# A hybrid decoder block: a second delta head's operands turned by VectorE and DMA in place of TensorE, and other numbers in the ordering

## The chip, the cores and the metric

One core of one Trainium2 chip. The metric is device microseconds of one execution of the whole program. The kernel before took 626.52 us in the median of three runs (623.9 to 627.73).

## The reference

The program computes one decoder layer in float32 for 1024 positions of width 1024. After an RMS norm, one projection gives the inputs of two groups of heads that work side by side: eight heads of stick-breaking attention (width 64) and four heads of a gated delta rule (width 128). Both groups' outputs are normed per head, gated, put beside each other, multiplied by one output matrix and added to the input, and a last RMS norm follows. The part that the change touches first is the delta rule, which works on chunks:

```python
qkv = jax.nn.silu(causal_depthwise_conv(concat([g_q, g_k, g_v]), gdn_conv_w))
gq, gk = l2norm(to_heads(gq)), l2norm(to_heads(gk))
# per chunk: k_beta = k * beta, v_beta = v * beta, decay from the cumulated g
a_mat = where(strict, einsum('bhnid,bhnjd->bhnij', k_beta, k) * decay, 0)
sol = triangular_solve(a_mat + eye, [v_beta, k_beta * exp(g)])
attn_intra = where(incl, einsum('bhnid,bhnjd->bhnij', q, k) * decay, 0)
# scan over chunks: v_new = u - w S;  o = (q exp(g)) S + attn_intra v_new
# S = S exp(g_last) + (k exp(g_last - g))^T v_new
```

The other part is the norm of the attention's output, `o_sb = rmsnorm(o_sb, sb_norm_w) * silu(sb_z)`, ahead of the output product.

## The kernel before, in words

**Tiles.** Positions are cut into 8 blocks of 128, the width into 8 of 128. Every large product is made as three products of float32 parts (a high and a low part of each operand, high x high, high x low, low x high; `mm3`, line 615), each 128x128 by 128x512 where it can be.

**Stages.** First the queries of the attention and its values are projected, with the input's split into high and low parts. Then two kinds of work share TensorE: the rest of the projections, which serve as filler, and the chains of the attention heads and of the delta heads. Then comes the output: the delta group's half of the product first (`products_delta`, line 1617), block by block, then the attention's half with the last norm (`products_attention`, line 1643).

**A delta head.** The projections of k, q and v of a delta head h (names G{h}1, G{h}0 and G{h}2) come out with the channel on the partitions and the position along the free side, 512 positions at a time; `g_evac` (line 913) applies the convolution and the gate. The inner products need them in this form, but the norms, the state's update and the solve need them turned, with the position on the partitions. There are two ways to turn them, chosen by `h < TURNED` (line 32, value 2). Heads below it keep k and q on the chip: GpSimd's product writes them straight into the operand tile kq, and v is stored to DRAM (g_s) and loaded again as it is; `gdn_pre` (line 1087) then turns all three by TensorE transposes against a unit matrix into PSUM, four of 128x128 for each of k, q and v of a unit (a unit is one half of the sequence of one head, four chunks). ScalarE squares the result, VectorE copies k out of PSUM, ScalarE scales v. Heads from it on are turned on the way: VectorE transposes each 128x512 block in squares of 32 (tile tn), four DMAs store its quarters to DRAM (gt_s) so that the squares land in turned order, and k and q are also stored unturned (g_s). `delta_load` (line 1036) loads kq from g_s, and the turned k, q and v (kn, nkv, vt) from gt_s; ScalarE's squares and scaling then read SBUF. All loads and stores of these go through SyncE's queue.

**The delta chain.** `gdn_pre` of both units, `gdn_sub` (line 1159, a forward substitution on GpSimd), `gdn_inv` (line 1192, the inverse of the 128x128 triangles in steps, tile xinv) and `gdn_chain` (line 1269, the scan over chunks) follow one another for each head. Units are numbered u = 2h + g. The operand tiles have room for four units, so unit u waits for the scan of unit u - 4. A unit's load of v waits until the unit before it is through with `gdn_pre`, and the loads of the next unit's k and q come behind it.

**The output.** `enter_delta` (line 1566) asks for the delta group's output blocks and their gates (tile mg), the first four as soon as the scan of unit 6 is through, and notes block b as ("in", b, 1) in `ready`. `out_norm` (line 1463), in two streams, one for even and one for odd blocks, loads the attention's output (tile both, four DMAs per block), adds its two parts, and makes the norm's factor; `enter_attention` (line 1630) uses it once all delta blocks have been asked for.

**What sets the order.** The program is written out as some twenty streams (`interleave`, line 468; the list stands at the end of `block`). A model of the chip (`Model`, line 188) runs beside the writing: each instruction has a cost, and the time at which its result can be used elsewhere is its end plus a hop (`HOPS`, line 41: A is ScalarE, G GpSimd, P TensorE, V VectorE, S the DMAs; `TO_PE`, line 42, is added where TensorE is the reader). A stream may go on when what it waits for has ended by the model's clock plus the hop, `TO_PE` and `SLACK` (line 465):

```python
return all(o.end is not None and o.end + HOPS[o.eng] + TO_PE + SLACK <= ck.now for o in self.waits)
```

Of the streams that may go on, the one with the best priority writes its next TensorE instructions; the other engines' orders come from the model's heaps by priority. In the end each engine's instructions are tied into this order. So these numbers set no wait on the chip; they set who stands behind whom.

Of the kernel before, what the change touches and what calls it, by code (L numbers as in the profile page):

```python
# [17 lines left out]
P = 128  # L18
# [4 lines left out]
SBH = 8  # L23
# [5 lines left out]
ORDER = "G0 v1 k0 G1 k1 G2 k2 G3 k3 z4 z5 z6 z7 z0 z1 z2 z3".split()  # L29
LOADS = "k0 k1 x0 k2 x1 x2 k3 x3 x4 k4 x5 k5 x6 x7 k6 k7 c0 c1 c2 c3 s c4 c5 c6 c7".split()  # L30
WINDOWS = 3
TURNED = 2

# [2 lines left out]


SAME = 130  # L40
HOPS = {"A": 145, "G": 75, "P": 197, "V": 130, "S": 900}
TO_PE = 70
SLACK = 450
GAP = "gap"

PORT = 60
# [141 lines left out]
class Model:  # L188
# [95 lines left out]
    def hop(self, d, op):  # L284
        return SAME if d.eng == op.eng != "S" else HOPS[d.eng] + (TO_PE if op.eng == "P" else 0)

# [14 lines left out]
    def finish(self, op):  # L301
        op.end = self.now
        for u in op.users:
            self.wake(u, op.end + self.hop(op, u))
        self.at(op.end + HOPS[op.eng] + TO_PE + SLACK, lambda: None)

# [147 lines left out]
class Stream:  # L454
# [7 lines left out]
    def ready(self, ck):  # L462
        if self.gate and not self.gate():
            return False
        return all(o.end is not None and o.end + HOPS[o.eng] + TO_PE + SLACK <= ck.now for o in self.waits)

# [35 lines left out]
def block(tc, xT_d, x_d, n1_d, wE_d, wQ_d, wC_d, conv_d, alog_d, dtb_d, mixw_d, wo_d, fnw_d, out_d):  # L502
    nc = tc.nc
    ck = Model({"V": nc.vector, "A": nc.scalar, "G": nc.gpsimd, "P": nc.tensor, "S": nc.sync})
    V, A, G, TE, S = ck.V, ck.A, ck.G, ck.P, ck.S

    with ExitStack() as top:
# [7 lines left out]
        fx = Fixed(ck, nc, {**{f"sg{w}": (2048 * (w + 1), 1) for w in range(4)}, "o2": (1024, 1), "kq": (4096, 4), "ak": (4096, 4)})  # L515
# [29 lines left out]
        def rsqrt(y, a, n):  # L545
            return G.tensor_tensor(y, a, half[:, 0:n], ALU.pow)
# [33 lines left out]
        def turned(tp, parts):  # L580
            ck.hold(tp)
            for u, a in enumerate(parts):
                if a.dtype == F32R:
                    TE.transpose(tp[:, u * P:(u + 1) * P].bitcast(F32R), a, idr)
                else:
                    TE.transpose(tp[:, u * P:(u + 1) * P], a, ident)
            ck.free(tp)
            yield from ()
# [161 lines left out]
        def first(f, *args, bank=BANK, **kw):  # L750
            ck.prio, prio = bank, ck.prio
            f(*args, **kw)
            ck.prio = prio
# [49 lines left out]
        flags = {}  # L803
# [103 lines left out]
        def operand(h, g):  # L907
            if (h, g) not in operands:
                operands[h, g] = fx.tile([P, 4, 2, P], F32, "kq", "kq")
                ck.hold(operands[h, g])  # L910
            return operands[h, g]

        def g_evac(h, kind):
# [3 lines left out]
            def evac(pt, half):  # L917
# [14 lines left out]
                ts = slice(half * 512, half * 512 + 512)  # L932
                if h < TURNED and kind < 2:
                    kq = operand(h, half)
# [4 lines left out]
                first(G.tensor_tensor, ac, ac, sg, ALU.mult)  # L939
                if h < TURNED:  # L940
                    return S.dma_start(g_s[h, kind, :, ts], ac)
# [94 lines left out]
        def delta_load():  # L1036
            yield lambda: "dec" in flags
            for h in range(GH):
                for g in range(2):
# [9 lines left out]
                    for kind in (1, 0):  # L1049
                        yield lambda: f"G{h}{kind}{half}" in flags  # L1050
                        loads.append(flags[f"G{h}{kind}{half}"] if h < TURNED else S.dma_start(kq[:, :, 1 - kind, :], g_s[h, kind, :, ts].rearrange("p (c t) -> p c t", c=4)))
                    ak = fx.tile([P, 2, 4, P], F32, "ak", "ak")
# [4 lines left out]
                    turned = lambda kind: gt_s[h, kind, ts, :].rearrange("(c t) d -> t c d", t=P)  # L1057
                    if h >= TURNED:
                        loads += [S.dma_start(kn, turned(1)), S.dma_start(nkv, turned(0))]
                    flags[f"l{u}g"] = loads  # L1060
                    yield lambda: f"G{h}2{half}" in flags and (u == 0 or f"q{u - 1}" in flags)
                    vt = gd.tile([P, 4, P], F32 if h >= TURNED else F32R, tag="vt", name="vt")
                    flags[f"v{u}g"] = S.dma_start(vt, turned(2)) if h >= TURNED else S.dma_start(vt.rearrange("p c t -> p (c t)").bitcast(F32), g_s[h, 2, :, ts])
                    gst[h, g].update(vt=vt)
# [396 lines left out]
        normed = {}  # L1461

        def out_norm(n):
            yield lambda: f"e{SBH - 1}3" in flags and fx.room("sg3")
            if n == 0:
                fx.part("sg3", 4096)
            for b in range(n, NB, 2):
                yield lambda: fx.room("sg3")
                both = fx.tile([P, SBH, 2, SBD], F32, "both", "sg3")
                ck.hold(both)  # L1470
                loads = []
                for q in range(4):
                    at = 32 * (4 * (b % 2) + q)
                    loads.append(S.dma_start(both[32 * q:32 * q + 32].rearrange("p h u d -> p (h u d)").rearrange("p (n c) -> p n c", c=32),
                                             o_s[b // 2, :, :, at:at + 32].rearrange("h (a r) c -> r (h a) c", r=32)))
                yield loads
                yield lambda: ck.now > max(op.end for op in loads) + 2000
                o, spare = both[:, :, 0, :], both[:, :, 1, :]
                V.tensor_tensor(o, o, spare, ALU.add)
                A.activation(spare, o, AF.Square)  # L1480
                ss = at_.tile([P, SBH], F32, tag="oss", bufs=2, name="oss")
                V.tensor_reduce(ss, spare, AX.X, ALU.add)
                V.tensor_scalar(ss, ss, 1.0 / SBD, EPS, ALU.mult, ALU.add)
                rsqrt(ss, ss, SBH)
                normed[b] = both, o, ss
                yield
# [74 lines left out]
        ready = {}  # L1561
# [81 lines left out]
        def products_attention():  # L1643
            yield lambda: f"d{NB - 1}" in flags
            for b in range(NB):
# [3 lines left out]
                for got in product(b, 0, parts):  # L1649
# [41 lines left out]
        interleave(ck, lambda: ps.room("pz", 4),  # L1691
                   [Stream(delta_scan(), 0, DELTA), Stream(delta_solve(), 0.5, DELTA + 0.5), Stream(delta_substitute(), 0.6, DELTA + 0.6),
                    pre, Stream(delta_load(), 0.4, DELTA + 0.4), Stream(attention(), 9.995, WINDOW), Stream(attention_values(), 9.99, WINDOW), Stream(out_rows(), 9.1, OUT_WEIGHTS), Stream(out_weights(), 9, OUT_WEIGHTS), Stream(out_weights_attention(), 9.25, OUTPUT + 1), Stream(out_rest(), 9.26, OUTPUT + 1), Stream(enter_x(), 9.31, OUTPUT - 4), Stream(out_norm(0), 9.15, OUTPUT - 1), Stream(out_norm(1), 9.16, OUTPUT - 1), fill,
                    Stream(enter_delta(), 9.3, OUTPUT - 4), Stream(prepare(1), 9.2, OUTPUT), Stream(products_delta(), 101, OUTPUT - 5),
                    Stream(enter_attention(), 9.1, OUTPUT - 3), Stream(prepare(0), 9.05, OUTPUT - 2), Stream(products_attention(), 102, OUTPUT - 1.5)])
# [39 lines left out]
```

## Time and profile before

| what | value |
|---|---|
| median of three runs | 626.52 us (623.9 to 627.73) |
| the profiled execution's own time | 624.59 us |
| its span, first to last instruction | 622.9 us |
| granted TensorE clock, mean | 0.998 |
| moved by DMA | 115.99 MB, mean 186 GB/s |

The profile is one execution. Its rows give, for each engine, the busy time, and for a group of like instructions their count, total busy time, mean duration and the idle time of the engine ahead of them. PE is TensorE, PEld its weight loads, DVE VectorE, ACT ScalarE, POOL GpSimd, SPq the issuing of DMAs in SyncE's queue. Matmuls overlap: the pace of TensorE is read from one start to the next and not from durations. In the table of stages the columns are the stretch, its length, busy time and count of each engine in the order PE, PEld, DVE, ACT, POOL, then the granted clock, the DMA engines' busy share and GB/s. Nearly all instructions carry the line of the recording helper (L377), so rows are told apart by the tiles that they write and read: kwf is the operand tile read by the transposes of k and q, vt that of v, akf the turned k, pz and pp are PSUM.

### The profile page before, as it was taken

The page shows a single profiled execution, that of the slowest core. Times are in us where ns is not written, and L with a number is a line of the kernel's source. Part 1 is how long each engine was busy: PE and PEld are TensorE (multiplying, and loading weights), DVE is VectorE, ACT ScalarE, POOL GpSimd, SP SyncE. Part 2 cuts the span into 40 slices and gives each one's busy share as a digit, 9 for nine tenths or more (in the row PEclk, how much of TensorE's full clock was granted, in tenths as well). Part 3 has the DMA queues.
Part 4 walks back from the last instruction along what each step waited for, and adds up shares of the span by engine and source line. Part 5 has one row for each costly group of instructions (what it writes and reads, how often), then busy time and mean ns, then how long its engine had stood idle before and what let it go on. Part 6 is the DMA issues. An engine that isn't in the chain of part 4 may idle for free.

```text
span 622.9 us, 11147 instructions
## 1 busy us (share of the span) xinstructions
PE 611.9 (98%) x3672; PEld 518.2 (83%) x3672; DVE 445.2 (71%) x803; ACT 397.1 (64%) x971; POOL 346.6 (56%) x435
## 2 busy tenths in 40 slices
PE   8999999999999999999999999999999999999995
PEld 7889988998888888887888888788878888888785
DVE  4369983242587787889789787886998865567774
ACT  5765468833776786885878767766778743223554
POOL 0126043945887469786558796584854416325433
PEclk9999999999999999999999999999999999999999
DMA  8968234776226547678647789236454389997632
GB/s 292 336 227 316 85 124 131 255 258 218 70 87 218 175 125 210 143 199 241 188 124 209 176 234 322 74 127 197 106 155 132 113 225 257 301 234 174 162 126 102
DMA packets 162233, 115.99 MB, mean 186 GB/s; under 512 B 95168, under 2 KB 130176, under 8 KB 162176
## 3 DMA queue, kind: packets, MB, share of 16 engines
q1 hardware_dynamic: 161888, 115.09, 61.3%
q8 instruction: 29, 0.48, 0.3%
q14 instruction: 28, 0.23, 0.1%
q10 hardware_dynamic: 288, 0.20, 0.1%
HBM read 78.12 MB, written 37.13 MB: 185 GB/s over the span
## 4 chain that ended last, share of the span: by engine, by line
PE 89%; ACT 2%; DVE 2%; DMA 2%; issue 2%; SPq 1%; POOL 1%; POOLq 0%; ACTq 0%
PE pp L377 57%; PE pz L377 23%; PE po L377 6%; PE pc L377 3%; DMA xr1f<-xT 1%; SPq L377 1%; DMA br<-bd 1%; ACT ahl L377 0%; ACT wy L396 0%; DVE xr L377 0%; POOL oss L377 0%; DVE xinv L396 0%; DVE mgf L377 0%; DVE oss L377 0%; DVE tn L377 0%
## 5 line engine op out<-in xcount | busy, mean ns | idle before, releaser
L377 PE MATMUL pp<-xh,weh 128*128 128x512 f32 x360 | 145.1, 403 | 0.0
L377 PE MATMUL pp<-xh,wel 128*128 128x512 f32 x360 | 140.8, 391 | 0.0
L377 PE MATMUL pp<-xl,weh 128*128 128x512 f32 x360 | 140.7, 391 | 0.0
L377 POOL TENSOR_TENSOR sgf<-sgf,cc 128x128 f32<-128x128 f32 (+3 forms) x64 | 77.2, 1210 | 54.5 <-DVE cc L377 43.2
L377 POOL TENSOR_TENSOR wel<-wer,weh 128x512 fp32r<-128x512 f32 x48 | 63.1, 1318 | 60.1 <-ACT weh L377 58.6
L377 PEld LDWEIGHTS pp<-xh,wel 128*128 128x128 f32 x360 | 67.6, 188 | 14.9
L377 PEld LDWEIGHTS pp<-xh,weh 128*128 128x128 f32 x360 | 67.7, 188 | 12.0
L377 PEld LDWEIGHTS pp<-xl,weh 128*128 128x128 f32 x360 | 67.8, 188 | 11.8
L377 ACT ACTIVATE sgf<-pz,rs 128x384 f32<-128x384 f32 (+3 forms) x96 | 53.7, 588 | 8.1 <-PE pz L377 7.7
L377 DVE TENSOR_TENSOR ahl<-pz,ahl 128x512 fp32r<-128x512 f32 (+1 forms) x80 | 49.5, 629 | 12.6 <-ACT ahl L377 12.0
L377 DVE TENSOR_TENSOR_SCAN cc<-pz,step 128x384 f32<-128x384 f32 (+2 forms) x64 | 53.4, 844 | 6.7 <-ACT pz L377 5.1
L377 ACT ACTIVATE pz<-pz,ns 128x384 f32<-128x384 f32 (+3 forms) x96 | 52.0, 569 | 0.0
L377 ACT ACTIVATE ahl<-pz 128x512 fp32r<-128x512 f32 (+1 forms) x80 | 43.1, 555 | 12.7 <-PE pz L377 12.4
L377 PE MATMUL po<-ahl,v2a 128*128 128x512 f32 (+1 forms) x160 | 49.3, 400 | 0.0
L377 PE MATMUL pp<-wo,mmf 128*128 128x512 f32 x192 | 44.5, 391 | 0.0
L377 POOL TENSOR_TENSOR mmf<-mgf,mmf 128x512 fp32r<-128x512 f32 x16 | 21.6, 1349 | 40.2 <-ACT mmf L377 40.2
L377 DVE SCALAR_TENSOR_TENSOR pp<-pre,conv,pp 128x512 f32<-128x512 f32 x42 | 31.4, 747 | 17.1 <-ACT pp L377 16.6
L377 PE MATMUL pp<-woh,mmf 128*128 128x512 f32 (+2 forms) x136 | 41.8, 382 | 0.4 <-ACT mmf L377 0.4
L377 PEld LDWEIGHTS pp<-wo,mmf 128*128 128x128 f32 x192 | 35.8, 188 | 7.4
L377 DVE TENSOR_TENSOR_SCAN cc<-pz,cc,step 128x512 f32<-128x512 f32 (+1 forms) x32 | 38.6, 1205 | 2.4 <-ACT pz L377 1.5
L377 PE MATMUL pz<-kh,q 128*128 128x384 f32 (+3 forms) x96 | 36.0, 382 | 0.9 <-DVE cc L377 0.3
L377 DVE TENSOR_TENSOR xr<-pp,xr 128x512 f32<-128x512 f32 (+2 forms) x33 | 22.2, 672 | 20.2 <-PE pp L377 18.1
(317 smaller groups left out, 1503.0 us busy)
## 6 DMA issues: line engine op xcount, KB each, us to landing
wer<-wE SPq DMA_DIRECT2D x48, 256.0 KB, 3.7
xr<-x SPq DMA_DIRECT2D x16, 512.0 KB, 6.4
v_s<-v2e SPq DMA_DIRECT2D x16, 256.0 KB, 3.0
v2a<-v_s SPq DMA_DIRECT2D x16, 256.0 KB, 2.9
q<-qk_s SPq DMA_DIRECT2D x8, 512.0 KB, 5.7
kh<-qk_s SPq DMA_DIRECT2D x8, 512.0 KB, 4.9
kl<-qk_s SPq DMA_DIRECT2D x8, 512.0 KB, 5.8
o_s<-oe SPq DMA_DIRECT2D x32, 128.0 KB, 3.5
```

What stands on the lines that cost most here:

```text
L377: ins = f(*args, **kw).ins
```

## The change

```diff
-TURNED = 2
+TURNED = 1
...
-HOPS = {"A": 145, "G": 75, "P": 197, "V": 130, "S": 900}
-TO_PE = 70
-SLACK = 450
+HOPS = {"A": 150, "G": 75, "P": 197, "V": 120, "S": 900}
+TO_PE = 80
+SLACK = 435
...
         def out_norm(n):
-            yield lambda: f"e{SBH - 1}3" in flags and fx.room("sg3")
+            yield lambda: f"e{SBH - 1}3" in flags and fx.room("sg3") and ("in", 1, 1) in ready
```

With `TURNED` at 1, head 1 goes the way of heads 2 and 3: only head 0 is still turned by TensorE. The streams of the attention's norm start only when the delta group's output blocks 0 and 1 have been asked for. Four of the model's numbers differ, two up and two down.

## The prediction

> **What bounds the kernel now.** I read the page first (busy shares, granted clock, the chain that ended last), then the table of stages, then the timeline of TensorE around the instructions that go, then the groups by shape.
>
> ```profile
> span 622.9 us, 11147 instructions
> ...
> PE 611.9 (98%) x3672; PEld 518.2 (83%) x3672; DVE 445.2 (71%) x803; ACT 397.1 (64%) x971; POOL 346.6 (56%) x435
> ...
> PE 89%; ACT 2%; DVE 2%; DMA 2%; issue 2%; SPq 1%; POOL 1%; POOLq 0%; ACTq 0%
> ```
>
> ```profile
> 150.00:220.00 70.00, 70.00 (x454) 57.96 (x453) 49.09 (x87) 49.24 (x131) 50.34 (x69) 1.00 0.41 137
> 220.00:290.00 70.00, 69.45 (x407) 58.81 (x407) 60.30 (x107) 53.21 (x146) 55.96 (x76) 1.00 0.69 187
> ...
> 210.00:460.00 250.00, 248.49 (x1622) 209.37 (x1623) 208.03 (x383) 183.92 (x499) 176.54 (x243) 1.00 0.62 177
> ...
> 617.00:623.00 6.00, 0.00 (x0) 0.00 (x0) 0.71 (x2) 1.07 (x3) 1.12 (x2) 0.75 0.33 128
> ```
>
> TensorE is the bound: 98% busy over the span, 89% of the chain that ended last, no idle time at all from 150 to 220 us and 1.51 us of 250 from 210 to 460 us; the granted clock is 1.00 until the tail. The last 6 us, without TensorE, are the last block's norm and store, which the change leaves alone. So an edit counts by what it takes off TensorE's queue or by the stalls it makes there; work on other engines counts only if TensorE ends up waiting for it.
>
> **The change, part by part.** *Head 1's transposes leave TensorE.* The loops over heads use "h < TURNED", so with 1 in place of 2 only head 1 (units 2 and 3, its two halves of the sequence) changes its path. Per unit 4 transposes of k, 4 of q and 4 of v go, 24 in all; the rows below are those of head 1.
>
> ```profile
> 173.18 0.80 PE L377 MATMUL pz<-step,kwf 128*128 128x128 f32 x8
> 173.81 0.46 PE L377 MATMUL pp<-xh,weh 128*128 128x512 f32 x1
> ...
> 206.13 0.54 PE L377 MATMUL pz<-step,vt 128*128 128x128 f32 x4
> 206.50 0.84 PE L377 MATMUL pz<-step,kwf 128*128 128x128 f32 x8
> 207.18 0.70 PE L377 MATMUL po<-ahl,v2a 128*128 128x512 f32 x2
> ...
> 214.90 0.53 PE L377 MATMUL pz<-step,vt 128*128 128x128 f32 x4
> 215.27 0.70 PE L377 MATMUL po<-ahl,v2a 128*128 128x512 f32 x2
> ```
>
> One group's price is its start to the start of what follows, since starts show the pace and durations overlap: 173.81 - 173.18 = 0.63, 207.18 - 206.13 = 1.05, 215.27 - 214.90 = 0.37, together 2.05 us for 24, or 0.085 us each. As this stretch has no idle time, all of it is on the bounding engine: -2.05.
>
> [...]
>
> *What VectorE gets.*
>
> ```profile
> L377 DVE STREAM_TRANSPOSE tn<-ac 128x512 f32<-128x512 f32 x12 | 8.4, 698 | 0.5 <-POOL ac L377 0.5
> ...
> L377 DVE COPY akf<-pz 128x512 f32<-128x512 f32 x4 | 2.7, 683 | 0.5 <-DMA dt_s<-dtf 0.5
> ```
>
> Twelve transposes of a 128x512 block serve heads 2 and 3, six per head (three kinds, two halves). Head 1 adds six: 6 x 0.698 = 4.2 us. Two copies of the turned k out of PSUM go: 2 x 0.683 = 1.4. Net +2.8 us on VectorE, which is 49.09 of 70 busy in the stage where they fall; the cover is its 20.9 us of idle time there. ScalarE's squares and scalings are the same in number, reading SBUF in place of PSUM. GpSimd's products keep their number too.
>
> *What SyncE's queue and the DMA engines get.* Before, head 1 issues 4 DMAs (v stored and loaded twice). After: 4 stores of k and q, 24 stores of turned quarters, 4 loads of k and q, 4 of their turned forms, 2 of v: 38, so 34 more.
>
> ```profile
> g_s<-ac SPq DMA_DIRECT2D x12, 256.0 KB, 2.5
> gt_s<-tn SPq DMA_DIRECT2D x48, 64.0 KB, 2.8
> ...
> akf<-gt_s SPq DMA_DIRECT2D x4, 256.0 KB, 4.7
> ...
> L377 SPq DMA_DIRECT2D gt_s<-tn x48: 303/490/1457, 220.5 to 357.7; - x48
> ```
>
> At the median of 0.49 us for one issue this is 34 x 0.49 = 16.7 us more in the queue. Blocks go up by 16 x 256 KB = 4.2 MB; with the 9.6 MB moved from 150 to 220 (70 us at 137 GB/s) that is 13.8 MB, or 197 GB/s, near the 187 of the next stage, where heads 2 and 3 already go this way. That stage is the nearest row for all the side effects together. It shows 0.55 us of TensorE idle per 70, and slower issue of the first matmul after a wait:
>
> ```profile
> L377 PE MATMUL pp<-xh,weh 128*128 128x512 f32 x70 | 27.6, 395 | 0.0
> ...
> L377 PE MATMUL pp<-xh,weh 128*128 128x512 f32 x58 | 23.5, 406 | 0.0
> ```
>
> These are 150 to 220 and 220 to 290 us. If head 1's stage became like the next, it would lose 0.55 + 70 x 0.011 = 1.3 us; if the queue has room, 0; six freed PSUM banks (one for each group of four transposes) allow a gain, bounded by the 0 idle of the stage to nothing visible. VectorE comes to 51.9 of 70, a quarter of the way from 49.1 to 60.3, so I take a quarter: +0.3.
>
> *Is head 1 late?* Its operands now pass through DRAM.
>
> ```profile
> 188.03 1.30 POOL L377 TENSOR_TENSOR ac<-ac,pre 128x512 f32<-128x512 f32 x1
> ...
> 201.34 0.32 SPq L377 DMA_DIRECT2D vt<-g_s  x1
> ...
> 341.82 1.29 POOL L377 TENSOR_TENSOR ac<-ac,pre 128x512 f32<-128x512 f32 x1
> ...
> 350.60 0.37 SPq L377 DMA_DIRECT2D vt<-gt_s  x1
> ```
>
> From the product of v to the issue of its load it is 13.3 us in head 1 (not turned) and 8.8 in head 3 (turned), so v is no later than now. Unit 3's k and q are loaded behind unit 2's v: issue near 201.3, four issues of 0.49, landing 4.7: 208.0. Today unit 3's turning starts at 206.50 and ScalarE's squares some 0.7 later; so unit 3 is about 1 us late. The next thing that could be late is head 1's substitution, then its scan, which frees the buffers of head 3's units. Two covers stand there.
>
> ```profile
> 455.65 0.44 DVE L377 STREAM_TRANSPOSE wc<-xc 128x256 f32<-128x256 f32 x1
> ...
> 459.68 0.40 ACT L377 ACTIVATE xinv<-xc 32x256 f32<-32x256 f32 x1
> ...
> 514.85 1.28 POOL L377 TENSOR_TENSOR mmf<-mgf,mmf 128x512 fp32r<-128x512 f32 x1 [3.81 <-ACT mmf L377]
> ...
> 524.52 0.39 PE L377 MATMUL pp<-xh,wel 128*128 128x512 f32 x1
> 524.75 1.52 PE L377 MATMUL pp<-wo,mmf 128*128 128x512 f32 x6
> ```
>
> Head 3's inverse is at hand at 455.65 and used at 459.68: 4.0 us. The output's first block is split at 514.85 + 1.28 = 516.13 and TensorE, filled with projections until then, takes it at 524.75: 8.6 us. Cost of 1 us of lateness: 0; without these covers, 1.
>
> *The norms' loads wait.* The added condition holds back the first loads of the attention rows until the output's second block has been asked for.
>
> ```profile
> 502.53 0.38 SPq L377 DMA_DIRECT2D bothf<-o_s  x1
> ...
> 504.00 0.46 SPq L377 DMA_DIRECT2D bothf<-o_s  x1
> 504.51 3.22 SPq L377 DMA_DIRECT2D mgf<-og_s  x1
> ...
> 508.80 0.44 SPq L377 DMA_DIRECT2D mgf<-gate_s  x1
> ...
> L377 DVE TENSOR_TENSOR mgf<-bothf,oss x8: 681/682/1351, 539.2 to 604.1; 128x512 f32<-128x512 f32 x8
> ```
>
> Two loads stand ahead of the second block's today; they move behind 508.80, some 6.7 us later, and at most the other six loads of these two blocks with them. Queued behind the condition is only the norm's own chain, whose result is first wanted at 539.2; and the first output block comes at most 2.0 us (504.51 - 502.53) earlier into an 8.6 us wait. Both ends are covered: 0. Without cover it would be +6.7 or -2.0.
>
> *Hop times.* They are numbers of the planner that writes each engine's order, and put no instruction on the chip. The time after which a stream may go on is the sum of three: after ScalarE 145 + 70 + 450 = 665 and 150 + 80 + 435 = 665; after VectorE 650 and 635; after GpSimd 595 and 590. The order is new all the same, since 34 DMAs come and 24 transposes go. Its worth cannot be read ahead; its bound can:
>
> ```profile
> L377 PE MATMUL pp<-xh,weh 128*128 128x512 f32 x360 | 145.1, 403 | 0.0
> ...
> L377 PE MATMUL pp<-xl,weh 128*128 128x512 f32 x360 | 140.7, 391 | 0.0
> ...
> L377 PE MATMUL po<-ahl,v2a 128*128 128x512 f32 x128 | 45.5, 430 | 0.0
> ```
>
> Against 391 ns, the two slow groups lose 360 x 0.012 + 128 x 0.039 = 9.3 us, and 1.5 us of idle stand from 210 to 460: an order without a stall would gain 10.8, one twice as poor would lose as much. I take 0, as nothing points to either side.
>
> **The sum**: -2.05 + 0.3 + 0 + 0 + 0 = -1.75. The profiled execution took 624.59 (its span 622.9 and 1.7 around it), which gives 622.84. The median of the three runs is 626.52, 1.93 above it; the new one will be compared as a median, so I add half of that: 623.8.
>
> **The rivals.** *The new order pays* (B): half of the 10.8 us of stalls goes. For it: they are made of waits between engines, which the order sets. Against it: nothing in the change aims at a named one. 624.59 - 1.75 - 5.4 + 0.97 = 618.4, faster by 1.3%. *Head 1 comes late* (C), the side of slower: SyncE's queue is in order, 24 stores each wait for a VectorE transpose, and what stands behind them, head 1's own loads among them, waits too. The lateness goes from unit 3 through head 1's scan to head 3's loads and to the output's first block, and decides from 4.0 + 8.6 = 12.6 us on; from there each us costs one. At 22 us (all 16.7 of issue time and one landing of 4.7 in series) it costs 8.8: 624.59 - 1.75 + 8.8 + 0.97 = 632.6. For it: single issues of up to 1.457 us. Against it: heads 2 and 3 are served in 8.8 us. [...] *Nothing comes of it* (D): other work closes the gaps at once and TensorE waits elsewhere for as long: 624.59 + 0.97 = 625.6. Against it: no idle time around the 24.
>
> **How the numbers follow.** Forecast 0.60, B 0.20, C 0.11, D 0.09. One per cent, 6.3 us, is about what a measurement of this kernel tells from no change. B alone is faster by more, C alone slower, the other two lie within: 0.20, 0.69, 0.11. The range runs from 616.5 (B with a little more than half of its stalls) to 632.5 (C at its price); outside it I leave a third of B and half of C with the tails of the rest, under 0.2.
>
> **What would show it.** Right: the group of transposes of kwf falls from 32 to 16 and of vt from 16 to 8, the turned blocks rise from 12 to 18 and their stores from 48 to 72, TensorE's busy time falls by about 2 us with its idle time unchanged. The norms' loads stand behind the second output block, and the first product still follows the last projection without a gap. Wrong: a gap there (C); mean durations of the two slow groups moved by 10 ns or more (B, or its opposite); TensorE's busy time the same (D).

## The result, and the profile after

The changed kernel takes 629.50 us in the median of 20 runs (625.43 to 632.59), the kernel before 626.24 in as many beside it (623.6 to 628.53, and one slow run of 676.07 that the ratio leaves out): ratio 1.0056, 95% interval 1.0038 to 1.0073, so slower by 0.6%. The prediction said 623.8, and 616.5 to 632.5 as its range: the time lies within the range and on the other side of no change.

The profiled execution took 628.0 us. From its page (span, busy times, granted clock in 40 slices, the chain that ended last):

```profile
span 626.3 us, 11173 instructions
...
PE 611.0 (98%) x3648; PEld 518.4 (83%) x3648; DVE 451.4 (72%) x807; ACT 398.8 (64%) x971; POOL 345.9 (55%) x435
...
PEclk9999999999999899999999999999999999999999
...
PE 82%; DVE 7%; ACT 4%; POOL 2%; issue 2%; DMA 1%; SPq 0%; POOLq 0%; DVEq 0%; ACTq 0%
```

TensorE is 0.9 us less busy than before (611.9), and the span is 3.4 us longer, so its idle time has grown by 4.3 us: 15.3 where before had 11.0. The chain runs through VectorE for 7% of the span (2% before). And one slice of the granted clock, the fourteenth (203 to 219 us), reads 8 and not 9. The table of stages says where the idle time went. After, then before:

```profile
200.00:210.00 10.00, 7.79 (x127) 5.94 (x125) 9.24 (x20) 9.26 (x33) 6.21 (x9) 1.00 0.60 144
210.00:220.00 10.00, 9.88 (x55) 8.07 (x55) 6.08 (x16) 4.65 (x14) 2.35 (x6) 0.83 0.58 196
...
400.00:410.00 10.00, 8.32 (x126) 6.18 (x126) 9.00 (x20) 7.75 (x19) 5.75 (x6) 1.00 0.32 89
470.00:490.00 20.00, 18.55 (x175) 15.13 (x174) 18.23 (x32) 15.76 (x40) 8.88 (x9) 1.00 0.38 111
515.00:600.00 85.00, 85.00 (x400) 70.49 (x399) 55.85 (x88) 30.02 (x61) 36.07 (x27) 1.00 0.83 224
```

```profile
200.00:210.00 10.00, 10.00 (x133) 8.35 (x132) 7.75 (x17) 8.46 (x34) 4.03 (x8) 1.00 0.76 256
...
400.00:410.00 10.00, 9.77 (x53) 8.18 (x54) 8.97 (x17) 6.61 (x17) 7.60 (x11) 1.00 0.44 143
470.00:490.00 20.00, 19.86 (x113) 16.22 (x111) 17.25 (x32) 15.33 (x37) 10.02 (x8) 1.00 0.28 94
515.00:600.00 85.00, 84.46 (x389) 69.29 (x388) 56.41 (x88) 30.86 (x57) 37.36 (x29) 1.00 0.83 216
```

Three short stretches hold most of it: 2.2 us of TensorE's idle time at 200 to 210 (none before), 1.7 at 400 to 410 (0.2 before), 1.45 at 470 to 490 (0.1). The output has none. The three are the inverses of heads 0, 2 and 3. At the first of them VectorE (third busy column) has gone from 7.75 to 9.24 of 10 us, and the ten us behind it have a granted clock of 0.83.

The timeline shows it instruction by instruction. The inverse passes three times from TensorE to VectorE and back: TensorE's first products (wc, dt) are copied into y, the second (xc, y) into wy and xinv, and the third (wy, dt) read these. VectorE after, at head 0's inverse:

```profile
205.23 0.86 DVE L377 COPY y<-pz 32x256 f32<-32x256 f32 x2
206.12 1.22 DVE L377 TENSOR_TENSOR_SCAN cc<-pz,step 128x512 f32<-128x512 f32 x1
207.38 0.42 DVE L377 COPY wy<-pz 32x256 f32<-32x256 f32 x1
207.81 0.85 DVE L377 COPY xinv<-pz 32x256 f32<-32x256 f32 x2
```

and TensorE after:

```profile
207.62 0.28 PE L377 MATMUL pz<-kl,q 128*128 128x256 f32 x1
208.80 0.69 PE L377 MATMUL pz<-wy,dt 128*64 128x64 f32 x16 [0.90 <-DVE xinv L377]
210.12 0.50 PE L377 MATMUL pp<-xh,weh 128*128 128x512 f32 x1 [0.64 <-DVE kt L377]
210.46 0.39 PE L377 MATMUL pp<-xl,weh 128*128 128x512 f32 x1
210.69 0.46 PE L377 MATMUL pp<-xh,wel 128*128 128x512 f32 x1
210.95 0.63 PE L377 MATMUL pp<-xh,weh 128*128 128x512 f32 x1
211.38 0.63 PE L377 MATMUL pp<-xl,weh 128*128 128x512 f32 x1
...
213.94 0.56 PE L377 MATMUL pp<-xl,weh 128*128 128x512 f32 x1
214.34 0.39 PE L377 MATMUL pp<-xh,wel 128*128 128x512 f32 x1
```

VectorE goes from one instruction to the next without a pause, an attention scan of 1.22 us stands ahead of the copies, and TensorE's third products wait for them (the bracket: idle time and what ended it). Then comes what the page's 8 stands for: from 210.95 to 213.94 the same 128x512 products start 0.43 us apart where they start 0.23 apart before and after it. The granted clock is 0.50 for 3.4 us there (210.90 to 214.30), which costs an estimated 1.7 us (half of 3.4). Before, VectorE had pauses there, and TensorE had head 1's transposes to run ahead of the second products (the rows from 206.13 to 207.18 that the prediction shows) and twelve projection products behind them. VectorE, then TensorE, before:

```profile
206.25 0.86 DVE L377 COPY y<-pz 32x256 f32<-32x256 f32 x2 [0.53 <-PE pz L377]
...
208.57 0.42 DVE L377 COPY wy<-pz 32x256 f32<-32x256 f32 x1 [0.98 <-PE pz L377]
209.00 0.85 DVE L377 COPY xinv<-pz 32x256 f32<-32x256 f32 x2
```

```profile
208.44 0.54 PE L377 MATMUL pz<-step,stf 128*128 128x128 f32 x4
208.81 0.46 PE L377 MATMUL pp<-xh,weh 128*128 128x512 f32 x1
...
211.43 0.39 PE L377 MATMUL pp<-xh,wel 128*128 128x512 f32 x1
211.75 0.69 PE L377 MATMUL pz<-wy,dt 128*64 128x64 f32 x16
```

So VectorE's results are not later than before: the copies of xinv end at 208.66 after and at 209.85 before. TensorE comes to them sooner. Between its second and its third products it has two small ones after (from 207.40 and 207.62 on) and sixteen before, so after the change it stands ready for xinv at 207.90 and waits, while before it came to it at 211.75.

**The clock goes with the time.** The mean granted clock of the 20 runs lies between 0.986 and 0.997, mean 0.9915; in 23 runs of the kernel before it is 0.9973. One stretch of 3.4 us at 0.50 in 627, as in the profiled run, lowers the mean by 0.0027; by this estimate the lower mean is worth some two such stretches in a run (the profiled run, at 0.995, has one). (0.9973 - 0.9915) x 629.5 = 3.7 us, where the medians differ by 3.3: by this estimate the change would be worth about -0.4 us without these stretches. The 20 runs are one kernel in one order, and their times go with their clocks: the five at 0.995 or more took 625.4 to 628.3 us, the seven at 0.989 or less 630.3 to 632.0. A run with longer waits may have both, so this alone does not say what the clock costs by itself.

### The profile page after: what moved, and what is told of

Same layout as the page of the kernel before. It is cut to its first block, busy times and chain, and to the rows that moved or that the text cites. A ratio compares the mean times of both kernels' runs of the same rounds, so it can differ in the third digit from the quotient of the medians.

```text
span 626.3 us, 11173 instructions
## 1 busy us (share of the span) xinstructions
PE 611.0 (98%) x3648; PEld 518.4 (83%) x3648; DVE 451.4 (72%) x807; ACT 398.8 (64%) x971; POOL 345.9 (55%) x435
## 4 chain that ended last, share of the span: by engine, by line
PE 82%; DVE 7%; ACT 4%; POOL 2%; issue 2%; DMA 1%; SPq 0%; POOLq 0%; DVEq 0%; ACTq 0%
PE pp L377 55%; PE pz L377 20%; PE po L377 5%; PE pc L377 3%; DVE cc L377 2%; DMA wq<-wQ 1%; ACT sgf L377 1%; POOL sgf L377 1%; ACT pz L377 1%; DVE ahl L377 1%; POOL tm L377 0%; ACT akf L377 0%; POOL xs L377 0%; DVE pp L377 0%; POOL wel L377 0%
## 5 line engine op out<-in xcount | busy, mean ns | idle before, releaser
L377 PE MATMUL pp<-xh,weh 128*128 128x512 f32 x360 | 146.6, 407 | 0.6 <-DVE kt L377 0.6
L377 PE MATMUL po<-ahl,v2a 128*128 128x512 f32 (+1 forms) x160 | 47.9, 396 | 0.0
L377 DVE TENSOR_TENSOR xr<-pp,xr 128x512 f32<-128x512 f32 (+2 forms) x33 | 22.2, 673 | 21.2 <-PE pp L377 20.9
```

The lines of the kernel that those rows point to most:

```text
L377: ins = f(*args, **kw).ins
```

## The experiments

Theory 1: TensorE's short waits at the delta heads' inverses, bunched within some microseconds, are followed by half-clock stretches, and these are the loss. Theory 2: the half clock has another origin and the new order costs the time as work and waits on the path; or any new order falls where it falls. All numbers are medians; every ratio is against the kernel before on the same chip. "Busy" is TensorE's busy time between 203 and 213 us in the run's own profile, around head 0's inverse (in e10 and e10b its third products start only at 220.85 and 216.19 us). "Between" is the number of products that TensorE has there between the inverse's second and third products, fillers included, by each run's timeline.

| kernel | TURNED | other | us | ratio, 95% interval | clock | busy | between |
|---|---|---|---|---|---|---|---|
| before | 2 | old hops, slack 450 | 626.24 | 1 | 0.998 | 10.00 | 16 |
| changed | 1 | new hops, slack 435, gate | 629.50 | 1.0056 (1.0038 to 1.0073) | 0.991 | 7.67 | 2 |
| e1 | 1 | as before | 644.38 | 1.0282 (1.0247 to 1.0318) | 0.990 | 8.08 | 2 |
| e2 | 2 | new hops, 435 | 628.51 | 1.0036 (1.0017 to 1.0055) | 0.997 | 10.00 | 20 |
| e4 | 1 | new hops, 435, no gate | 635.64 | 1.0145 (1.0112 to 1.0178) | 0.989 | 7.60 | 2 |
| e7 | 2 | before + 24 transposes | 626.23 | 1.0006 (0.9986 to 1.0027) | 0.997 | 10.00 | 16 |
| e8 | 1 | changed + 24 filler products | 630.33 | 1.0078 (1.0060 to 1.0097) | 0.998 | 8.95 | 6 |
| e9 | 2 | before + 24 filler products | 629.78 | 1.0071 (1.0047 to 1.0095) | 0.998 | 10.00 | 20 |
| e11 | 1 | changed + 8 filler products | 629.57 | 1.0055 (1.0030 to 1.0081) | 0.993 | 8.22 | 4 |
| e12 | 2 | before + late copies | 630.43 | 1.0061 (1.0036 to 1.0086) | 0.995 | 10.00 | 16 |
| e10 | 1 | changed, solves 800 ns later | 635.32 | 1.0162 (1.0139 to 1.0186) | 0.991 | 5.94 | 14 |
| e10b | 2 | before, solves 800 ns later | 637.09 | 1.0184 (1.0165 to 1.0203) | 0.988 | 10.00 | 10 |
| a 425 | 1 | changed, slack 425 | 628.57 | 1.0041 (1.0017 to 1.0065) | 0.994 | 7.66 | 2 |
| a 440 | 1 | changed, slack 440 | 629.67 | 1.0063 (1.0036 to 1.0091) | 0.991 | 7.86 | 2 |
| a 450 | 1 | changed, slack 450 | 636.59 | 1.0159 (1.0116 to 1.0203) | 0.985 | 7.56 | 2 |
| a 460 | 1 | changed, slack 460 | 637.85 | 1.0196 (1.0164 to 1.0228) | 0.992 | 7.34 | 0 |
| b 440 | 2 | before, slack 440 | 635.48 | 1.0145 (1.0099 to 1.0192) | 0.998 | 9.97 | 20 |
| b 445 | 2 | before, slack 445 | 623.97 | 0.9965 (0.9942 to 0.9989) | 0.997 | 10.00 | 16 |
| b 455 | 2 | before, slack 455 | 627.21 | 1.0021 (0.9998 to 1.0044) | 0.998 | 10.00 | 16 |
| e13 | 1 | changed, head 1's turns as copies | 629.66 | 1.0063 (1.0043 to 1.0083) | 0.993 | 8.03 | 2 |

### The parts of the change

e1 has the turning alone, e2 the numbers of the ordering alone, e4 both without the gate. The gate by itself has no run: added to the kernel before, to e1 or to e2, it leaves every engine's written order as it is. Only with TURNED at 1 and the new numbers together does it move instructions. So e2 is also the changed kernel with TURNED at 2.

```diff
# e1
-TURNED = 2
+TURNED = 1
# e2
-HOPS = {"A": 145, "G": 75, "P": 197, "V": 130, "S": 900}
-TO_PE = 70
-SLACK = 450
+HOPS = {"A": 150, "G": 75, "P": 197, "V": 120, "S": 900}
+TO_PE = 80
+SLACK = 435
# e4: both
```

> The change's first part alone: head 1 turned by VectorE, old hop times, no gate. Theory (order): the loss of the changed kernel is made of stalls where the new order puts the inverse's matmuls of a delta head too close behind the VectorE copies that they read, and of half-clock windows of 3.4 us that follow such stalls; it hangs on the order, so this kernel, with another order, may come out anywhere from 1.75 us below the kernel before (stalls as before) to 4 us above. Rival (turning): the added VectorE and queue work costs 3 us whatever the order: 629 to 630 us, as the changed kernel, with waits in the stretch from 160 to 220 us. A clock of 0.997 or more with a time under 626 speaks for the order, one of 0.992 or less with a time near 629.5 for either, and then the place of the waits decides.

> The hop times alone: head 1 still turned by TensorE. Theory (order): another order of the same work, so the time moves by the stalls it happens to make, within 4 us of the kernel before to either side, and the granted clock tells how many half-clock windows it met, about 1.5 us for each 0.0027 of mean clock. Rival (turning): hop times are harmless, ratio 1.000 within 0.002.

> Head 1 turned by VectorE and the new hop times, without the gate on the norms' loads. Both theories: as the changed kernel, ratio 1.0056 within 0.003, if the gate does nothing until the output; the waits at the inverse near 205 to 210, 404 to 408 and 478 to 481 us stand there again. If it is level with the kernel before or faster, the gate has a price after all, of 3 us.

The turning alone costs 18 us, far outside what either theory gave it. TensorE's longest wait in e1 (us in all, times, the longest), and the stage with it:

```profile
PE pp L377 <- POOL wel L377: 4.3, 1, 4.3
```

```profile
365.00:380.00 15.00, 10.72 (x54) 8.78 (x53) 8.48 (x13) 5.45 (x18) 13.01 (x15) 0.89 0.79 260
```

With the old numbers, the order that comes out of TURNED = 1 has TensorE wait 4.3 us in one piece for a weight's low part from GpSimd at 371 us, and a clock of 0.89 over these 15 us. In all TensorE is idle for 23.4 us in e1 (11.0 before), and three slices of its granted clock read 8 (0.991 in the mean of the profiled run). The new numbers take 8.7 us off (644.38 to 635.64), the gate another 6.1 (to 629.50). This too was not expected (ratio 1.0056 within 0.003). In e4 the last attention rows are asked for at 599.5 us (594.1 in the changed kernel), and the last block waits for its halves. Two of TensorE's waits there, and the stage:

```profile
605.69 0.50 PE L377 MATMUL pp<-woh,mmf 128*128 128x512 f32 x1 [1.24 <-ACT mmf L377]
...
607.34 1.22 PE L377 MATMUL pp<-woh,mmf 128*128 128x512 f32 x2 [0.92 <-POOL mmf L377]
```

```profile
600.00:612.00 12.00, 9.82 (x41) 7.42 (x40) 7.41 (x15) 5.57 (x11) 5.46 (x5) 0.86 0.45 125
```

That is 2.2 us of idle time and a clock of 0.86 over the 12 us; in the changed kernel TensorE has no idle time from 590 to 612. It is not the whole of the 6.1 us, and the clock on record does not follow e4's times throughout: one of its six runs shows 0.943 and is the fastest, 632.94 us. So the small edits mend orders that the first one upset; alone, the numbers cost 2.3 us (e2), with the clock at 0.997 and TensorE's waits in the output (busy for 81.49 of 85 us from 515 on). Set against e2, which differs in TURNED alone, the changed kernel is slower by 0.0056 - 0.0036 = 0.0020, or 1.3 us (-0.4 to 2.9): with these numbers the turning's own share is not clear of nothing.

### Does the removed work count?

e7 issues each of head 1's 24 transposes twice, in the order of the kernel before.

```diff
                     for which in range(2):
+                        if h == 1:
+                            nc.tensor.transpose(tp[...], kw[:, j, which, :], idr)
...
+                    if h == 1:
+                        nc.tensor.transpose(bank[...], vt[:, j, :], idr)
```

> The kernel before with each of head 1's 24 transposes on TensorE issued twice, every engine's order otherwise the same. It measures the term of 2.05 us by itself: on the path that sets the end, 2.0 us more, ratio 1.0033; hidden by waits, ratio 1.000. The first copies have names of their own line in the profile.

The pairs start 0.085 us apart, as the prediction read it, yet 24 more cost 0.4 us at the end (-0.9 to 1.7), and not 2.05. Its stage is as full as before's (the row of before stands in the prediction), so what they take there must be given back later in the run; where, no run shows.

```profile
150.00:220.00 70.00, 70.00 (x469) 58.31 (x468) 48.27 (x85) 48.35 (x129) 48.75 (x68) 1.00 0.42 135
```

### Filling the waits

e8 and e9 put two 512-column products ahead of the inverse's first product into its PSUM bank and four ahead of the next, which overwrite their results; the planner doesn't know of them, so the order stays. e11 has two per inverse, both in the second place.

```diff
             x1p = pz()
+            for _ in range(2):
+                nc.tensor.matmul(x1p, idr, stepr, start=True, stop=True)
...
             y2p = pz()
+            for _ in range(4):
+                nc.tensor.matmul(y2p, idr, stepr, start=True, stop=True)
```

> The changed kernel with six extra 512-column matmuls per delta head at the head's inverse (two ahead of the first product into the inverse's bank, four ahead of the second's), their results overwritten: 24 matmuls, 5.4 us of TensorE work at 0.227 us each, put where TensorE waits for VectorE's copies. Theory 1 (short waits bunched at the inverses are followed by 3.4 us at half clock, each worth 1.7 us, about two and a half of them in a run): the mean clock goes from 0.991 back to 0.996 or more and the time falls from 629.5 us to 625.5 to 628, below the changed kernel in spite of the added work. Theory 2 (the half-clock stretches have another origin): the clock stays near 0.991 and the time is 629.5 to 635. Theory 3 (the changed order is slower by work on the path, the clock is only a companion): the time rises by the added 2 to 5.4 us whatever the clock does.

> The same 24 extra matmuls in the kernel before, whose mean clock is 0.998: the control that prices them. Theory 1: no half-clock stretches are there to be saved, the clock stays at 0.997 to 0.998, and the time rises by 2 to 5.4 us to 628 to 631.6, less what falls into waits. Theory 2 and 3: the same rise as in the changed kernel.

> The changed kernel with only two extra 512-column matmuls per inverse, ahead of the product that waits for the second copies (8 in all, 1.8 us at 0.227 us each; in the kernel before the 24 of the earlier run cost 3.9 us, so 8 cost about 1.3). Theory 1 (the lost time is half-clock stretches behind bunched waits): they fill the longest wait of the bunch; the mean clock rises to 0.995 or more from 0.991, and the time is 626.5 to 628. Theory 2 (a companion): clock 0.991, time 630 to 631.

The clock does what theory 1 says: back to 0.998 from 0.991 in the changed kernel, unchanged in the kernel before. Two stretches of 3.4 us at head 0's inverse, in e8:

```profile
207.50:210.90 3.40, 2.35 (x60) 1.68 (x62) 2.33 (x6) 3.18 (x18) 2.50 (x4) 1.00 0.77 223
210.90:214.30 3.40, 3.40 (x30) 2.56 (x26) 1.90 (x4) 2.52 (x7) 1.18 (x5) 1.00 1.01 270
```

and in the changed kernel:

```profile
207.50:210.90 3.40, 1.86 (x21) 1.44 (x22) 2.46 (x6) 3.34 (x16) 2.78 (x6) 1.00 0.95 256
210.90:214.30 3.40, 3.40 (x9) 2.64 (x8) 1.25 (x2) 1.77 (x6) 0.32 (x2) 0.50 0.98 324
```

TensorE busy for 1.86 of 3.4 us is followed by a clock of 0.50, busy for 2.35 by 1.00. The time did not fall to 625.5 to 628, as I had expected it to: the filler costs more than it mends, 0.0071 x 626 = 4.4 us in the kernel before. In the changed kernel it costs 0.0078 - 0.0056 = 0.0022, or 1.4 us. The 3.1 us between them (0.9 to 5.3, from the three intervals) are what the filler mends in the changed kernel and not in the kernel before. That is not the clock alone, since waits shrink too: by the pages TensorE's idle time falls from 15.3 to 12.5 us in e8 and rises from 11.0 to 12.5 in e9. The clock by itself (0.9915 to 0.9968 in the mean) would give 3.3 as an estimate; these runs do not part the two. With the filler on both sides the change costs 0.0007 x 626 = 0.4 us (-1.5 to 2.3). e11's eight products raise the clock to 0.993 only; its two longest bunches stay, and the time with them. My expectation for it failed: the filler ran behind the wait and not within it. The two products at head 0 start at 208.78, after 0.89 us of waiting for xinv; in e8 the four in the second place start at 209.60, after 1.05.

### Making the kernel before late

```diff
+            for _ in range(3):
+                nc.vector.tensor_copy(W[32:64, :, 0:32], xv[32:64])
             r = V.tensor_copy(W[32:64, :, 0:32], xv[32:64])
```

> The kernel before with VectorE's copy of the second product made four times in place of once (three more, 0.42 us each, 1.26 us per inverse), unknown to the planner, so that every result behind it on VectorE lands 1.3 us late, as in the changed kernel where VectorE has no pause at 200 to 208 us. Theory 1 (late copies at the inverses make TensorE wait in bunches, and half clock follows): the clock falls from 0.998 to 0.988 to 0.994, and the time rises to 629 to 636: up to 1.3 us of waiting at each of four inverses, and 1.7 us for each half-clock stretch. Theory 2 (the half-clock stretches have another origin): clock 0.998, and the time rises by no more than the waits, 0 to 5 us.

```profile
290.00:298.00 8.00, 6.24 (x90) 4.83 (x89) 7.34 (x16) 5.42 (x13) 0.40 (x2) 1.00 0.88 285
394.00:400.00 6.00, 4.88 (x85) 3.43 (x83) 5.08 (x14) 2.59 (x7) 1.28 (x1) 1.00 0.22 55
462.00:469.00 7.00, 5.42 (x63) 4.28 (x58) 6.79 (x16) 5.45 (x15) 2.52 (x5) 1.00 0.12 31
```

```profile
290.00:298.00 8.00, 7.29 (x95) 5.67 (x95) 7.57 (x15) 5.78 (x14) 0.90 (x3) 1.00 0.85 252
394.00:400.00 6.00, 6.00 (x104) 4.67 (x104) 4.64 (x12) 3.78 (x10) 1.28 (x1) 1.00 0.26 68
462.00:469.00 7.00, 6.58 (x62) 4.83 (x61) 5.77 (x12) 6.09 (x15) 1.87 (x3) 1.00 0.35 73
```

The first fence is e12, the second the kernel before. Copies 1.3 us late add about 1.1 us of idle time at each of the last three inverses, 3.3 in all; head 0's inverse, with its filler at hand, takes none (busy 10.00 in the table). The time rises by 0.0061 x 626 = 3.8 us, which the waits all but account for, and the clock falls from 0.997 to 0.995, just short of the 0.988 to 0.994 that theory 1 asked for. The bunches are 1.1 to 1.8 us of idle time here, smaller than at head 0 in the changed kernel (2.2); so the clock's sign is theory 1's, and the effect weaker than I had set it; the time alone lies within theory 2's 0 to 5 us as well. Its profiled run, at 0.999, lost 0.001 x 627 = 0.6 us to the clock, less than the 1.7 of one half-clock stretch.

### The solves later in the order

e10 and e10b ask for 800 ns more ahead of every step of the solves.

```diff
+        self.slack = SLACK + (800 if prio == 0.5 else 0)
-        ... + TO_PE + SLACK <= ck.now for o in self.waits)
+        ... + TO_PE + self.slack <= ck.now for o in self.waits)
```

> The changed kernel, with the solves' products put 800 ns later in the written order behind what they wait for than the model asks, so that other products stand where TensorE now waits at the inverses. Theory 1 (the waits come from results that land later than the model has them, and are followed by half-clock stretches): the mean clock is 0.995 or more, and the time 625 to 628. Theory 2 (any new order falls anywhere within some per cent): the time lies anywhere between 622 and 640, and the clock goes with it.

> The kernel before with the same 800 ns in its solves. Theory 1: few such waits were there, so the clock stays at 0.997 to 0.998 and the time within 2 us of 626.2, unless the later solves make the output wait. Theory 2: anywhere between 622 and 640 us.

Both are slower than the kernel before by ten us or more: my expectations for theory 1 failed in both. The waits went elsewhere, in both to the output's start. e10b:

```profile
520.00:541.00 21.00, 14.82 (x49) 11.29 (x48) 10.03 (x16) 5.59 (x19) 6.37 (x7) 0.59 0.65 189
```

6.2 of 21 us idle at the output's start, and a clock of 0.59 over them: 17 us at half speed. Heads that come out later are paid for there, as the prediction's rival C had it, though here it is the solves that were put off.

### Is it the order or the turning?

SLACK alone is changed, at either division of work: 425, 440, 450 and 460 in the changed kernel (which has 435), 440, 445 and 455 in the kernel before (450). As an example a 440:

```diff
-SLACK = 435
+SLACK = 440
```

> The changed kernel with 440 ns of slack in the planner in place of 435: another written order of the same work. If the place of the instructions decides and not the turning, the time falls anywhere between 624 and 640 us, with a clock between 0.985 and 0.998. If the turning by itself crowds VectorE at the inverses whatever the order, the clock is 0.993 or less and the time 628 or more.

> The kernel before with 445 ns of slack in place of 450: another written order of the old division of work. If the order decides: anywhere between 624 and 640 us. If the turning crowds VectorE and the old division doesn't: the clock is 0.996 or more, and the time 625 to 629.

> The changed kernel with 425 ns of slack in place of 435: a third written order of its work. Theory T (turning head 1 on VectorE makes results late at the inverses in any order): a half-clock stretch at 205 to 216 us in the profile, a mean clock of 0.993 or less, 628 us or more. Theory O (each order falls where it falls): any time from 622 to 640 us, the clock with it, with no stretch common to the orders.

> The changed kernel with 450 ns of slack, the value of the kernel before: a fourth order of the changed work. Theory T: a half-clock stretch at 205 to 216 us, clock 0.993 or less, 628 us or more. Theory O: any time from 622 to 640 us.

> The kernel before with 440 ns of slack: a third order of the old division of work. Theory T: no half-clock stretch at 205 to 216 us, clock 0.996 or more, 623 to 628 us. Theory O: any time from 622 to 640 us, and a clock as low as in the changed kernel's orders as often as not.

> The kernel before with 455 ns of slack: a fourth order of the old division of work. Theory T: no half-clock stretch at 205 to 216 us, clock 0.996 or more, 623 to 628 us. Theory O: any time from 622 to 640 us.

> The changed kernel with 460 ns of slack: a fifth order of the changed work. Theory T: a half-clock stretch at 205 to 216 us in the profile, clock 0.993 or less, 628 us or more. Theory O: any time from 622 to 640 us.

Two things separate here. *Head 0's inverse* is a matter of the division of work. In the table, every kernel with TURNED = 1 loses at least 1.8 us of TensorE there (busy 8.22 or less of 10; 8.95 with 24 fillers), with old numbers or new, in eight written orders; none of the nine kernels with TURNED = 2 loses more than 0.03. From 203 to 213 us the granted clock is 0.83 to 0.89 in the profiles of all of the first but e8, e10 and a 425, where it is 1.00 as in all nine of the second.

The last column of the table says what the orders share. Apart from fillers and from e10, TensorE has at most 2 products between the inverse's second and third with TURNED = 1, and waits 0.89 to 1.48 us for xinv; with TURNED = 2 it has 10 to 20 there, and does not wait for it. (e10 has 14 and does not wait for it either; its idle time is 1.50 us for ahl at 206.9 and 2.14 for kt at 213.3.) A busy VectorE makes no such wait by itself. In e2 and b 440 it takes up the second products 1.87 and 1.81 us after TensorE has made them, and TensorE, with 20 products at hand, loses 0.03 us at most; in the changed kernel it takes them up after 0.49, in a 460 after 0.05, and there TensorE, with nothing at hand, waits the longest, 1.48. Why the planner leaves this place empty when head 1 is turned by VectorE is open.

In a 425 the same wait was not followed by half clock in the profiled run, though a later one was:

```profile
207.30:210.70 3.40, 1.85 (x22) 1.44 (x21) 2.34 (x7) 3.34 (x14) 2.76 (x7) 1.00 0.71 241
210.70:214.10 3.40, 3.40 (x29) 2.64 (x28) 1.81 (x4) 1.58 (x5) 0.07 (x1) 1.00 0.94 320
477.00:480.40 3.40, 1.94 (x21) 1.33 (x21) 3.23 (x8) 2.47 (x6) 1.54 (x1) 1.00 0.91 300
480.40:483.80 3.40, 3.40 (x22) 2.30 (x21) 2.37 (x3) 2.28 (x5) 0.95 (x1) 0.50 0.41 125
```

a 440 has a second stretch at head 2's inverse:

```profile
404.00:407.40 3.40, 2.00 (x22) 1.48 (x23) 3.28 (x9) 2.04 (x5) 0.70 (x1) 1.00 0.56 149
407.40:410.80 3.40, 3.40 (x9) 2.60 (x8) 1.89 (x4) 3.36 (x8) 0.00 (x0) 0.50 0.73 249
```

*The total time* is a matter of the order. It spreads over 628.6 to 644.4 us with TURNED at 1 and over 624.0 to 637.1 with 2. b 440 takes 635.48 us at a clock of 0.998 (so theory T, which gave it 623 to 628, missed, as the 625 to 629 for b 445 did), with 3.3 of 21 us idle at the output's start among its waits:

```profile
520.00:541.00 21.00, 17.73 (x87) 14.01 (x86) 12.36 (x20) 6.36 (x20) 10.52 (x9) 1.00 0.81 238
```

The best of each side are 628.57 (a 425) and 623.97 (b 445): the fastest kernel of the study, 0.35% below the kernel before (0.11 to 0.58%, and picked as the best of several), turns two heads by TensorE.

### The turn's own length

e13 keeps the changed kernel's order and makes head 1's six turns by a copy.

```diff
+            ins = (self.real.tensor_copy if name == "transpose" and getattr(self, "short", False) else f)(*args, **kw).ins
...
+                V.short = h == 1
                 first(V.transpose, sg, ac)
+                V.short = False
```

> The changed kernel in its own written order, but head 1's six turned blocks are made by a plain copy of the same 128x512 tile in place of the turn (so head 1's turned blocks hold the wrong layout): a copy should take some 0.35 us where the turn takes 0.70. One of the six, at 201 us, stands in the stretch in which VectorE has no pause ahead of head 0's inverse. If the turn's own length makes the copies late: TensorE's wait in the 3.4 us ahead of the half-clock stretch at 210.9 us falls from 2.1 to 1.8 us, that stretch goes, the mean clock rises from 0.991 to 0.993 to 0.995, and the time falls by 1 to 2 us to 627.5 to 628.5. If it is the order around it (the scan ahead of the copies) and not the turn's length: clock 0.991, 629.5 us within 0.7.

The group of these copies (least, median and longest in ns) and, from the timeline, the one at head 0's inverse:

```profile
L377 DVE COPY tn<-ac x6: 401/425/1423, 159.3 to 201.2; 128x512 f32<-128x512 f32 x6
```

```profile
201.19 1.05 DVE L377 COPY tn<-ac 128x512 f32<-128x512 f32 x1
```

The six copies have a median of 0.43 us (0.40 at the least; no run shows the 0.35 that I had expected), but the one that counts, at 201.19, took 1.05, longer than the turn that it stands for (0.70). So the test failed to shorten what it was to shorten: the time (629.66) and the wait at head 0 stay, and how much of that wait is the turn's own time is left open.

## Why the prediction was wrong, point by point

**Failed: the stage's side effects, +0.3 (bounds 0 to 1.3), with the new order put at 0.** This is the step. The prediction took the next stage as the nearest row and scaled its 0.55 us of idle time by how busy VectorE gets, with "its 20.9 us of idle time there" as the cover. VectorE's load came out as said; TensorE's idle time did not:

```profile
150.00:220.00 70.00, 67.67 (x426) 55.53 (x424) 51.46 (x91) 49.68 (x132) 49.59 (x68) 0.98 0.70 198
```

VectorE is 51.46 of 70 us busy (51.9 forecast) and the DMAs move 198 GB/s (197 forecast), yet TensorE idles for 2.33 us, all of it around head 0's inverse, and 3.4 us at a clock of 0.50 follow, an estimated 1.7 us. What decides there is not a share of a stage but what TensorE has at hand while VectorE copies: 16 products before, 2 in every order with TURNED = 1 but a 460, which has none, and e10 (fillers apart). The order was set to 0 "as nothing points to either side"; yet all the orders of the new division of work, e10 apart, leave this place nearly empty. That VectorE's turns make the wait is not shown: the copies of xinv end sooner than before.

**Failed with it: the granted clock was taken as 1.00 until the tail.** That row was true of before and was carried over to after. Waits of 0.9 us at most, 1.5 us of them within 3.4, were followed by 3.4 us at a clock of 0.50, which cost an estimated 1.7. By the clocks of the runs the change without it would have come out near nothing (-0.4, an estimate). How much of the 3.3 us is clock and how much the waits themselves stays open: the fillers (e8 against e9) mend 3.1 us of both together.

**Mis-sized: -2.05 for the transposes.** They are gone (16 of kwf and 8 of vt are left, 1.8 and 1.1 us busy), and their pace in the trace was read rightly. "As this stretch has no idle time, all of it is on the bounding engine" does not follow to the end: 24 more of them cost 0.4 us (e7). They were, besides, work that stood at 206 us between the inverse's steps. No run shows what their absence there does by itself; e2 has eight of them between the second and the third products, beside twelve projections.

**Head 1 late, 0: right.** The first output product follows the last projection without a gap, TensorE being busy for 85.00 of 85 us from 515 on. Head 1's first copies of xinv stand at 296.05 us, 2.2 later than before (293.89), with 4.0 us lost at head 0 ahead of it. Rival C did not come. (Its 8.8 us follow from 16.7 + 4.7 = 21.4 and not from the 22 that it names.)

**The norms' gate, 0: wrong in both halves.** It does not move two loads by itself, as the prediction had it: alone it changes nothing. And it is not worth 0 here: without it (e4) the changed kernel takes 6.1 us more, with new waits at the last output block and not at the first.

**Hop times, 0 with a bound of 10.8 us.** That their worth can't be read ahead is borne out by the orders' spread, and the bound was too small on the side of the loss: the turning with the old numbers lies 18 us above before, and the new numbers alone cost 2.3 (e2). The two slow groups barely moved (403 to 407 ns and 430 to 425), against rival B.

**By its own list of signs:** counts of kwf, vt, turned blocks (18) and their stores (72) are as said; TensorE's busy time fell by 0.9 and not 2, and its idle time did not stay but grew by 4.3. That last sign had no rival behind it: short waits of TensorE at the inverses were not among the four cases.

## What to carry to other kernels

Where the bounding engine needs a result back from another one, count what it has at hand until then, in stretches of some microseconds; here neither the idle sum of a stage nor the other engine's busy share told whether it would wait (VectorE 51.46 of 70 us busy as forecast, TensorE idle for 2.33). When a change can make the bounding engine wait in short pieces, price what its clock does behind them as well, and take the clock from the runs, not only from the profiled one. Where the order is written out by a planner, run several orders of each version before an edit is credited or blamed: here one and the same division of work spans 13 us.

## What the runs showed of the hardware

In the changed kernel the half clock came without a long pause: single waits of 0.9 us at most, adding up to 1.5 us in a stretch of 3.4, were followed by 3.4 us at half speed (busy 1.86 of 3.40, then a clock of 0.50); 2.35 us busy, in e8, were not (then 1.00). Below 2.35 the stretches shown go either way: 2.00 was followed by 0.50 in a 440 and 1.94 in a 425, while 1.85 was followed by 1.00 in the same run of a 425. The longest gap between TensorE's instructions in the changed kernel is 1.7 us, at the start, and 0.9 at the inverses. The 20 runs of this one kernel differ in their mean clock (0.986 to 0.997); what makes them differ no run shows.

On VectorE, a copy of one 128x512 block from SBUF to SBUF took between 0.40 and 1.42 us in one execution of e13 (median 0.43, and 1.05 for the one at 201.19 us), while the turns of the same shape stayed between 0.68 and 0.71. What stretched the longest copies was not tried.
